# Two feature tiles to one output tile and store at the end of a decoder block, c loaded first and a shorter chain in its head

## The chip, the cores and the metric

The kernel runs on one core of one Trainium2 chip. The metric is the device time of one execution in microseconds, as the median of several runs. A core has five engines with queues of their own: PE (TensorE, matmuls), DVE (VectorE), ACT (ScalarE, activations and table lookups), POOL (GpSimd) and SP (SyncE, which in this kernel issues DMAs). Each runs its own instructions in order and waits for the others by semaphores.

## The reference

One sequence of 1024 tokens with 1024 features goes through one block in fp32. `c` is one vector of 1024 values, which conditions every norm:

```python
c_act = silu(c)
cond = c_act @ ada_w + ada_b                      # shift1, scale1, gate1, shift2, scale2, gate2
h = modulate(rmsnorm(x, norm1_g), shift1, scale1)
u, v, val, gate = split(h @ w_in + b_in)          # 512 columns each
y_a = spatial_gating_mixer(gelu(u), gelu(v), ...) # layernorm of v, 128x128 mixing in chunks
y_b = conformer_conv_mixer(val, gate, ...)        # causal depthwise conv of width 31, group norm, silu
x = x + gate1 * (concat(rmsnorm(y_a), rmsnorm(y_b)) @ w_out)
h2 = modulate(rmsnorm(x, norm2_g), shift2, scale2)
g, up = split(h2 @ w_ffn_in)
x = x + gate2 * ((silu(g) * up) @ w_ffn_out)
out = modulate(rmsnorm(x, norm_f_g), shift_f, scale_f)   # shift_f, scale_f from c_act @ ada_f_w + ada_f_b
```

## The kernel before

Features lie on the partitions and tokens along the free axis. x is held as `xs[k]`, eight feature tiles (k = 0 to 7) of 128 features by 1024 tokens, and most work goes by halves of 512 tokens (`H`). Each operand of a large matmul is split into two parts, hi and lo (`wh`, `wl`, `h[:, 0]`, `h[:, 1]`), and a product is made of three matmuls, hi by hi, lo by hi and hi by lo (`mm3`, `product`), each 128x128 by 128x512, which PE starts 0.227 us apart at full speed.

**The head.** SP loads x (first half, eight DMAs), c and the column constants (`cols`). PE broadcasts c to all partitions by two matmuls of 128x512 (line 538), ACT applies Silu (`cact`, line 539). The columns of the conditioning come from `ada_cols` (lines 549 to 559): a 512 KB tile of `ada` is loaded into a buffer (`ypad`), and DVE multiplies it by `cact` and sums each row into one column of `cond` (line 559). `rstd` (lines 631 to 661) makes 1/rms: ACT squares the tiles of x (line 641), PE sums them over features into a bank `ssq` (line 648), ACT takes the root `rt` (line 651), DVE the reciprocal (652), PE spreads it over all partitions, back into the same bank (654), and where `copy` is set ACT copies it into SBUF as `r` (660). The loop over k (line 718 on) loads the ada tiles of SCALE1 and SHIFT1 and the weights `wk[k]`, splits the weights (`wh_k` by ACT, line 586, `wl_k` by DVE, 587), finishes the two columns on ACT (722, 723) and makes h: t = x * r on DVE (725), Identity with scale and shift on ACT, in place (726), hi as a copy of t by ACT (728), lo = t - hi by DVE (729). Then 24 matmuls add this k to eight banks `p`.

**The body.** The gates, the convolution, the spatial mixer (`v`, with the scalings of `vn` in line 781; `gn`, the group norm of the convolution from `gsd`; `pm`, the mixing) and the output projection `po` follow; `ssq_b` and `rt_b` belong to the norm of the convolution's output `y_b`. After that come the FFN's two products (line 928).

**The tail.** The last norm goes by pieces: piece 0 is the first 512 tokens, pieces 1 and 2 are 256 tokens each. `square` sums squares (ACT 1204, PE 1196), `norm` makes the rstd (1225 to 1228), and `output(i)` makes each feature tile by one DVE operation (1244), one ACT operation (1246) and one store issued by SP (1247); two tiles of piece 0 go by POOL and ACT (1240 to 1242).

**What sets the order.** The program is built in the order of its text, and then `fix_order` orders the instructions of each engine anew: a planner (`Graph`, `Slots`, `Clock`, `forward`, `backward`) holds the dependences and schedules the whole by a list, with a modelled duration for each instruction (`duration`). An edge set by `issue_after` keeps an instruction behind another one. The order on each engine is fixed by what the planner's last pass gives.

Of the kernel before, what the change touches and what calls it, by code (L numbers as in the profile page):

```python
# [68 lines left out]
DMA_AHEAD = 0.5  # L69

# [54 lines left out]
def duration(s):  # L125
# [3 lines left out]
    if s.engine == "PE":  # L129
        n, m = s.writes[0].width, s.reads[1].width  # L130
        if not s.reads[0].f32:
            t = n / 512 * 0.2267
        elif n == 128:
            t = {128: 0.219, 32: 0.068}.get(m, 0.109)
        else:
            t = 0.857
        return t, t + 0.176, 0
# [34 lines left out]
class Graph:  # L172


    def __init__(self, instructions, edges, stacked, reusing):
        self.steps = []
        uses, live, tiles, order = {}, {}, {}, {}
        for ins in instructions:
# [3 lines left out]
            for operands, written in ((s.reads, False), (s.writes, True)):  # L182
                for o in operands:
# [129 lines left out]
class Clock:  # L313


    def __init__(self):
        self.free = dict.fromkeys(ENGINES, 0.0)
        self.port = self.queue = 0.0
        self.last, self.partial = None, False

    def run(self, s, t):
# [10 lines left out]
        if s.engine == "PE" and s.partial != self.partial:  # L332
            self.partial = s.partial
            t += 0.09 if s.partial else 0.12
# [20 lines left out]
def forward(g, rank):  # L355
# [7 lines left out]
    slots, clock, table = Slots(g), Clock(), None  # L363
# [17 lines left out]
    for _ in range(count):  # L381
# [21 lines left out]
        for n in s.after:  # L403
            need[n] -= 1
            same = g.steps[n].engine == e and not s.dma
            at[n] = max(at[n], (begin + s.issue if e == "PE" else end) if same else end + SIGNAL[e])
# [62 lines left out]
def block_kernel(ctx: ExitStack, tc: tile.TileContext, xT, c, ada, cols, vbias, bs, wsp,  # L469
# [161 lines left out]
    def rstd(srcs, n, name, groups, add_eng, copy=False, size=H, tmp=tmp, bank=None):  # L631
# [29 lines left out]
        return r  # L661
# [49 lines left out]
    r1a = rstd(x_half(0), D, "n1_0", (1,) * 8, None, True)  # L711
# [6 lines left out]
    for k in range(KD):  # L718
# [512 lines left out]
    def output(i, tiles=range(KD), by_pool=()):  # L1231
        bank, part = norm_banks[i], pieces[i]
        size = part.stop - part.start
        if by_pool:
            r = ev(f"r_nf{i}")[:, 0:size]
            A.activation(r, bank[:, 0:size], AF.Copy)
        for k in tiles:
            t = ev(f"of{i}_{k}")[:, 0:size]
            if k in by_pool:
                G.tensor_tensor(t, xs[k][:, part], r, op=ALU.mult)  # L1240
                A.activation(t, t, AF.Identity, bias=ccol(SHIFTF, k), scale=ccol(SCALEF, k))
                nc.sync.dma_start(out[k, :, part], t)
# [173 lines left out]
```

## Time and profile before

| | us |
|---|---|
| three runs, median | 996.74 |
| lowest, highest | 996.40, 1000.49 |
| the profiled execution, own time | 996.41 |
| its span | 994.4 |
| PE busy | 961.9 (97%) |
| DVE busy | 855.2 (86%) |
| ACT busy | 474.0 (48%) |
| POOL busy | 391.4 (39%) |

The span reaches from the first to the last recorded instruction or transfer of the profiled execution; the own time has the rest around it, 2.0 us, in it. Busy time of an engine is the sum over its instructions, registers, branches and DMA issues not counted. In the views below a line gives the start and the duration of neighbouring instructions of one kind ("x4" is four of them, and the duration is then of all four from the first start to the last end); the bracket at its end is the idle time of the engine ahead of it and what released it. "SPq" is SP issuing DMAs; 'sum' rows add the stretches.

### The profile page before, as it was taken

What the parts mean: (1) busy time and instruction counts of PE and PEld (TensorE: products, weight loads), DVE (VectorE), ACT (ScalarE), POOL (GpSimd) and SP (SyncE); (2) the same over time, 40 slices, a digit from 0 to 9 for tenths busy, and PEclk for the clock granted to TensorE, in tenths of its full rate; (3) what the DMA queues carried; (4) which work ended last, traced back from release to release, by engine and by line L of the source; (5) the groups of instructions that cost most, each with busy time, mean ns of one, the idle gap of its engine ahead of it and who ended that gap; (6) DMA issues with size and microseconds to landing.
All of it is one profiled execution on the core that took longest, in us unless ns stands there. A gap on an engine that the chain in (4) does not pass through costs nothing.

```text
span 994.4 us, 13218 instructions
## 1 busy us (share of the span) xinstructions
PE 961.9 (97%) x4645; PEld 773.6 (78%) x4645; DVE 855.2 (86%) x1197; ACT 474.0 (48%) x751; POOL 391.4 (39%) x232
## 2 busy tenths in 40 slices
PE   4999999999999999999999999999999999999994
PEld 2887777778878778888888877888887888888873
DVE  3969999999999444799999999998678989869946
ACT  6668467643484363564332332323337437236416
POOL 0037879755556111574445544445443100000121
PEclk9999999999999999999999999999999999999997
DMA  8983351524465515764677777677557838315104
GB/s 301 329 315 101 123 175 56 189 96 127 148 223 180 190 43 169 259 232 145 221 253 233 244 240 255 227 241 234 186 180 259 303 131 259 121 40 173 33 1 169
DMA packets 73667, 184.08 MB, mean 185 GB/s; under 512 B 8193, under 2 KB 10497, under 8 KB 73602
## 3 DMA queue, kind: packets, MB, share of 16 engines
q1 hardware_dynamic: 73602, 183.25, 55.6%
q8 instruction: 36, 0.59, 0.3%
q14 instruction: 29, 0.24, 0.1%
HBM read 142.06 MB, written 41.16 MB: 184 GB/s over the span
## 4 chain that ended last, share of the span: by engine, by line
PE 83%; DVE 10%; issue 2%; ACT 2%; DMA 1%; POOL 0%; SPq 0%; ACTq 0%; DVEq 0%; POOLq 0%
PE B L928 24%; PE C L928 14%; PE ah L928 11%; PE p L603 3%; PE po L603 3%; PE po L604 3%; PE po L605 3%; PE p L604 3%; PE p L605 3%; PE A L928 3%; DVE w_f L921 2%; PE v L604 2%; PE v L603 1%; PE pu L605 1%; PE v L605 1%
## 5 line engine op out<-in xcount | busy, mean ns | idle before, releaser
L928 PE MATMUL B<-h,w_f 128*128 128x512 f32 x816 | 190.8, 390 | 2.3 <-ACT x L1145 1.2
L928 PEld LDWEIGHTS B<-h,w_f 128*128 128x128 f32 x816 | 152.7, 188 | 36.4 <-DVE x L1147 3.1
L866 DVE SCALAR_TENSOR_TENSOR cv<-ypad,colt,cv 128x512 f32<-128x512 f32 x216 | 147.6, 745 | 0.5
L928 PE MATMUL B<-fa,w_d 128*128 128x512 f32 x528 | 125.5, 390 | 0.3 <-DVE x L1277 0.2
L928 PE MATMUL C<-h,w_f 128*128 128x512 f32 x528 | 123.6, 389 | 0.0
L928 PEld LDWEIGHTS B<-fa,w_d 128*128 128x128 f32 x528 | 98.8, 188 | 22.0 <-DVE x L1277 1.1
L928 PEld LDWEIGHTS C<-h,w_f 128*128 128x128 f32 x528 | 99.1, 188 | 20.6
L928 PE MATMUL ah<-h,wh_a 128*128 128x512 f32 x320 | 101.6, 395 | 0.5 <-ACT sg L673 0.5
L1209 POOL TENSOR_TENSOR sq_nf<-sq_nf,sq_nf 128x512 f32<-128x512 f32 x9 | 12.5, 1388 | 175.6 <-ACT sq_nf L1204 175.6
L920 ACT ACTIVATE w_d<-raw_d 128x512 fp32r<-128x512 f32 (+1 forms) x72 | 42.0, 593 | 83.0 <-PE B L928 34.0
L1170 POOL TENSOR_TENSOR x<-x,up 128x512 f32<-128x512 f32 x20 | 34.7, 1737 | 106.1 <-ACT x L1169 106.1
L587 POOL TENSOR_TENSOR wl_a<-raw_a,wh_a 128x1024 fp32r<-128x1024 f32 x20 | 49.2, 2461 | 67.8 <-ACT wh_a L586 57.7
L920 ACT ACTIVATE w_f<-raw_f 128x512 fp32r<-128x512 f32 x68 | 42.3, 627 | 68.4 <-PE B L928 41.6
L921 DVE TENSOR_TENSOR w_f<-raw_f,w_f 128x512 fp32r<-128x512 f32 x68 | 68.7, 1017 | 5.1 <-ACT w_f L920 5.0
L928 PEld LDWEIGHTS ah<-h,wh_a 128*128 128x128 f32 x320 | 59.9, 188 | 15.1 <-issue 1.4
L928 PE MATMUL C<-fa,w_d 128*128 128x512 f32 (+1 forms) x273 | 64.4, 384 | 0.0
L928 PE MATMUL ah<-h,wl_a 128*128 128x512 f32 x160 | 62.2, 390 | 0.0
L928 PEld LDWEIGHTS C<-fa,w_d 128*128 128x128 f32 x273 | 49.9, 188 | 11.0 <-issue 0.8
L921 DVE TENSOR_TENSOR fa<-a,fa 128x512 fp32r<-128x512 f32 x77 | 54.2, 743 | 1.7 <-ACT fa L920 1.7
L1277 DVE SCALAR_TENSOR_TENSOR x<-B,cond,x 128x512 f32<-128x512 f32 x48 | 35.6, 743 | 19.8 <-PE B L928 19.8
L920 ACT ACTIVATE fa<-a 128x512 fp32r<-128x512 f32 x77 | 46.0, 626 | 8.8 <-DMA a<-acts 5.7
L921 DVE TENSOR_TENSOR w_d<-raw_d,w_d 128x512 fp32r<-128x512 f32 (+1 forms) x72 | 47.8, 673 | 1.4 <-ACT w_d L920 1.4
(236 smaller groups left out, 2094.2 us busy)
## 6 DMA issues: line engine op xcount, KB each, us to landing
acts<-x SPq DMA_DIRECT2D x77, 256.0 KB, 3.1
a<-acts SPq DMA_DIRECT2D x77, 256.0 KB, 4.0
raw_f<-wf SPq DMA_DIRECT2D x32, 512.0 KB, 4.5
ada<-ada SPq DMA_DIRECT2D x24, 512.0 KB, 3.4
x<-ada SPq DMA_DIRECT2D x24, 512.0 KB, 3.8
raw_a<-wf SPq DMA_DIRECT2D x20, 512.0 KB, 3.8
ahead<-ahead SPq DMA_DIRECT2D x40, 256.0 KB, 3.0
ypad<-ada SPq DMA_DIRECT2D x16, 512.0 KB, 5.4
```

Of the source, the lines that this page charges most:

```text
L587: lo_eng.tensor_tensor(lo, raw, hi.bitcast(F32), op=ALU.subtract)
L603: PE.matmul(acc, shi, mhi, start=start, stop=False)
L604: PE.matmul(acc, slo, mhi, start=False, stop=False)
L605: PE.matmul(acc, shi, mlo, start=False, stop=stop)
L866: V.scalar_tensor_tensor(accs[j], src, wc, accs[j], op0=ALU.mult, op1=ALU.add)
L920: A.activation(dst[:, 0, :], src, AF.Copy)
L921: lo_eng.tensor_tensor(dst[:, 1, :], src, dst[:, 0, :].bitcast(F32), op=ALU.subtract)
L928: last_mm = PE.matmul(bank[:, cols], s, m[:, cols], start=first and p == 0 and i == 0, stop=p == n - 1 and i == 2, skip_group_check=True)
L1170: G.tensor_tensor(g0, g0, up0, op=ALU.mult)
L1209: G.tensor_tensor(sums[half], sums[half], t, op=ALU.add)
L1277: V.scalar_tensor_tensor(xs[k][:, part], bank[:, cols], ccol(GATE2, k), xs[k][:, part], op0=ALU.mult, op1=ALU.add)
```

## The change

Three things change. In `output`, two feature tiles of a piece of 256 columns share one tile of 512 columns (`row`), and one store writes both; the output in DRAM is laid out in blocks of 512 columns, (2*KD, 128, 512), and the host puts the blocks together. In the head, c is loaded first, and `issue_after(c_load)` keeps x and cols behind it on SP; `rstd` returns its bank as well as the copy, the first t reads the bank, and h's hi part is made by Identity from t directly, ahead of the Identity in place that lo needs. In the planner, the cost of a narrow fp32 matmul has another formula, PE's time is doubled where the stretch before was little active (`tensor`), PE's writes to one bank keep the order of the program, and a PE instruction's follower on PE starts from `clock.free`.

```diff
@@ duration
         if not s.reads[0].f32:
             t = n / 512 * 0.2267
-        elif n == 128:
-            t = {128: 0.219, 32: 0.068}.get(m, 0.109)
         else:
-            t = 0.857
+            k = s.reads[0].box[1] - s.reads[0].box[0]
+            t = {128: 0.219, 32: 0.068}.get(m, 0.109 if k > 64 else 0.055) * n / 128
@@ Graph
+            if s.engine == "PE":
+                if s.writes[0].name in bank:
+                    s.before.add(bank[s.writes[0].name])
+                bank[s.writes[0].name] = s.n
@@ Clock
+    def tensor(self, t, s):
+        if s.partial != self.partial:
+            self.partial = s.partial
+            t += 0.09 if s.partial else 0.12
+        w = int(t / CLOCK_WINDOW)
+        slow = 2 if self.throttled and self.active.get(w - 1, 0.0) < CLOCK_WINDOW / 2 else 1
+        end = t + slow * s.issue
...
+        self.free["PE"] = end
+        return t, t + slow * s.finish
...
-    slots, clock, table = Slots(g), Clock(), None
+    slots, clock, table = Slots(g), Clock(True), None
...
-            at[n] = max(at[n], (begin + s.issue if e == "PE" else end) if same else end + SIGNAL[e])
+            at[n] = max(at[n], (clock.free[e] if e == "PE" else end) if same else end + SIGNAL[e])
@@ block_kernel
-    nc.sync.dma_start(c_row[0:1, :], c)
+    c_load = nc.sync.dma_start(c_row[0:1, :], c).ins
     colt = const.tile([P, NCOL], F32, name="colt")
-    nc.sync.dma_start(colt, cols)
     xs = [const.tile([P, S], F32, name=f"x{k}") for k in range(KD)]
-    for k in range(KD):
-        nc.sync.dma_start(xs[k][:, hs(0)], xT[k, :, hs(0)])
+    with issue_after(c_load):
+        for k in range(KD):
+            nc.sync.dma_start(xs[k][:, hs(0)], xT[k, :, hs(0)])
+        nc.sync.dma_start(colt, cols)
@@ rstd
         A.activation(r, bank, AF.Copy)
-        return r
+        return bank[:, 0:size], r
@@ loop over k
-    r1a = rstd(x_half(0), D, "n1_0", (1,) * 8, None, True)
+    r1a_bank, r1a = rstd(x_half(0), D, "n1_0", (1,) * 8, None, True)
...
-        V.tensor_tensor(t, xs[k][:, hs(0)], r1a, op=ALU.mult)
+        V.tensor_tensor(t, xs[k][:, hs(0)], r1a_bank if k == 0 else r1a, op=ALU.mult)
+        h = h1[0][k] = act_tile(f"h1_0_{k}", 0)
+        A.activation(h[:, 0, :], t, AF.Identity, bias=ccol(SHIFT1, k), scale=ccol(SCALE1, k))
         A.activation(t, t, AF.Identity, bias=ccol(SHIFT1, k), scale=ccol(SCALE1, k))
-        h = h1[0][k] = act_tile(f"h1_0_{k}", 0)
-        A.activation(h[:, 0, :], t, AF.Copy)
         V.tensor_tensor(h[:, 1, :], t, h[:, 0, :].bitcast(F32), op=ALU.subtract)
@@ output
         size = part.stop - part.start
+        per_store = H // size
...
-            t = ev(f"of{i}_{k}")[:, 0:size]
+            if k % per_store == 0:
+                row = ev(f"of{i}_{k}")
+            t = row[:, k % per_store * size:(k % per_store + 1) * size]
...
-            A.activation(t, t, AF.Identity, bias=ccol(SHIFTF, k))
-            nc.sync.dma_start(out[k, :, part], t)
+                A.activation(t, t, AF.Identity, bias=ccol(SHIFTF, k))
+            if (k + 1) % per_store == 0:
+                nc.sync.dma_start(out[(0, KD, KD + KD // 2)[i] + k // per_store], row)
```

SP at the start of the program before: x tiles, c and cols, then the two ada tiles of k = 0 (`ypad`).

```order
L524 DMA x_76<-xT 128x512
L524 DMA x_77<-xT 128x512
L524 DMA x_78<-xT 128x512
L524 DMA x_79<-xT 128x512
L524 DMA x_80<-xT 128x512
L524 DMA x_81<-xT 128x512
L519 DMA c_row<-c 1x1024
L524 DMA x_82<-xT 128x512
L524 DMA x_83<-xT 128x512
L521 DMA colt<-cols 128x277
L554 DMA ypad_106<-ada 128x1024
L554 DMA ypad_107<-ada 128x1024
```

SP at the same place in the changed kernel.

```order
L540 DMA c_row<-c 1x1024
L576 DMA ypad_106<-ada 128x1024
L576 DMA ypad_107<-ada 128x1024
L545 DMA x_75<-xT 128x512
L545 DMA x_76<-xT 128x512
L545 DMA x_77<-xT 128x512
L545 DMA x_78<-xT 128x512
L545 DMA x_79<-xT 128x512
L545 DMA x_80<-xT 128x512
L545 DMA x_81<-xT 128x512
L545 DMA x_82<-xT 128x512
L546 DMA colt<-cols 128x277
```

c has moved from the seventh place to the first, the two ada tiles from the end to ahead of all of x, and cols to the end.

ACT in the head before, from the seventh square of x to the root: `sq_n` are the squares, `cact` the Silu of c in two halves, `rt_n` the root of the sums in the bank `ssq_n`.

```order
L641 ACTIVATE sq_n_0_6_156<-x_82 128x512
L539 ACT_TABLE_LOAD
L539 ACTIVATE cact<-c_97 128x512
L641 ACTIVATE sq_n_0_7_162<-x_83 128x512
L539 ACTIVATE cact<-c_100 128x512
L696 ACTIVATE vsel<-colt 128x1
L542 ACT_TABLE_LOAD
L542 ACTIVATE warm<-epst 128x1
L651 ACTIVATE rt_n_0_168<-ssq_n_0_119,epst 128x128
```

ACT from the start of the changed kernel to the second square.

```order
L561 ACT_TABLE_LOAD
L561 ACTIVATE cact<-c_97 128x512
L561 ACTIVATE cact<-c_100 128x512
L663 ACTIVATE sq_n_0_0_120<-x_75 128x512
L564 ACT_TABLE_LOAD
L564 ACTIVATE warm<-epst 128x1
L663 ACTIVATE sq_n_0_1_126<-x_76 128x512
```

Silu with its table has moved from between the last squares to ahead of the first, and the table for the root from behind the last square to behind the first; one of three table loads is gone. The other six squares and three small operations follow, then `rt_n`.

ACT at the first h before: `wh_k` are the hi parts of the weights, `r_n` the copy of the bank, `h_0_0` the hi part of h for k = 0.

```order
L586 ACTIVATE wh_k_193<-raw_k_191 128x1024
L660 ACTIVATE r_n_0_175<-ssq_n_0_119 128x512
L722 ACTIVATE cond<-cond,gain,colt 128x1
L726 ACTIVATE t_h_0_0_199<-t_h_0_0_199,cond 128x512
L586 ACTIVATE wh_k_235<-raw_k_233 128x1024
L728 ACTIVATE h_0_0_202<-t_h_0_0_199 128x512
```

ACT at the same place in the changed kernel, from the root on.

```order
L673 ACTIVATE rt_n_0_168<-ssq_n_0_119,epst 128x128
L608 ACTIVATE wh_k_193<-raw_k_191 128x1024
L682 ACTIVATE r_n_0_175<-ssq_n_0_119 128x512
L749 ACTIVATE h_0_0_201<-t_h_0_0_199,cond 128x512
L750 ACTIVATE t_h_0_0_199<-t_h_0_0_199,cond 128x512
```

`h_0_0` has moved ahead of the Identity in place and of the second `wh_k`, and is made from `t_h_0_0` as DVE left it.

DVE in the changed kernel from the reciprocal on, with the semaphores that each instruction waits for (`Activation` is ACT's).

```order
L674 RECIPROCAL rt_n_0_168<-rt_n_0_168 128x128 [waits Activation_49]
L609 TENSOR_TENSOR wl_k_194<-raw_k_191,wh_k_193 128x1024 [waits DMAHW4_49,Activation_49]
L747 TENSOR_TENSOR t_h_0_0_199<-x_75,ssq_n_0_119 128x512 [waits Activation_49]
L581 SCALAR_TENSOR_TENSOR ypad_108,cond<-ypad_108,cact 128x1024 [waits DMAHW5_49]
L581 SCALAR_TENSOR_TENSOR ypad_109,cond<-ypad_109,cact 128x1024 [waits DMAHW6_49]
```

The first t reads `ssq_n` where it read `r_n`; it stands ahead of an ada product (108) that stood ahead of it, and waits for ACT alone.

PE at the start of the output projection of `y_b` before, where `ssq_b` are the sums and `rt_b` the roots of its norm.

```order
L605 MATMUL po_2_3163<-y_a_2_2562,wh_o_2_3157 128x512
L648 MATMUL ssq_b_3092<-sq_b_0_3093,ones 32x128 x4
L603 MATMUL po_2_3163<-y_a_3_2567,wh_o_2_3157 128x512
L604 MATMUL po_2_3163<-y_a_3_2567,wl_o_2_3158 128x512
L605 MATMUL po_2_3163<-y_a_3_2567,wh_o_2_3157 128x512
L654 MATMUL ssq_b_3092<-rt_b_3108,colt 128x128 x4
L603 MATMUL po_0_3161<-y_b_0_3117,wh_o_0_3145 128x512
L604 MATMUL po_0_3161<-y_b_0_3117,wl_o_0_3146 128x512
```

PE at the same place in the changed kernel.

```order
L625 MATMUL po_2_3163<-y_a_2_2562,wh_o_2_3157 128x512
L626 MATMUL po_2_3163<-y_a_2_2562,wl_o_2_3158 128x512
L627 MATMUL po_2_3163<-y_a_2_2562,wh_o_2_3157 128x512
L625 MATMUL po_2_3163<-y_a_3_2567,wh_o_2_3157 128x512
L626 MATMUL po_2_3163<-y_a_3_2567,wl_o_2_3158 128x512
L676 MATMUL ssq_b_3092<-rt_b_3108,colt 128x128 x4
L627 MATMUL po_2_3163<-y_a_3_2567,wh_o_2_3157 128x512
L625 MATMUL po_0_3161<-y_b_0_3117,wh_o_0_3145 128x512
```

The sums (`ssq_b<-sq_b`) have moved ahead: they stand 14 rows before the spread of `rt_b` now, with 13 po between, where 3 stood, and one po has moved behind the spread.

In the rest of PE's order, the first `gn<-gsd` stands at row 529 (before 550) and the first `pm<-wt,vn` at 548 (before 554); PE changes between narrow fp32 matmuls and full ones 68 times (before 72). SP's last stores are eight of 128x512 for pieces 1 and 2 (before sixteen of 128x256).

## Rows read from the trace of the kernel before

**Rows 1.** Stretches: length, each engine's busy time, PEclk, DMA share, GB/s.

```profile
0.00:24.20 24.20, 10.94 (x76) 4.58 (x76) 8.89 (x16) 15.32 (x25) 0.49 (x8) 1.00 0.86 302
...
31.20:200.00 168.80, 168.80 (x942) 132.62 (x940) 158.36 (x234) 111.47 (x168) 113.66 (x62) 1.00 0.53 181
...
978.00:994.40 16.40, 2.31 (x18) 1.32 (x16) 10.22 (x21) 10.63 (x24) 2.50 (x2) 0.67 0.63 217
sum 994.40, PE 961.86 PEld 773.65 DVE 855.25 ACT 473.96 POOL 391.40; mean PE 96.19 PEld 77.36 DVE 85.52 ACT 47.40 POOL 39.14
```

**Rows 2.** Timeline of ACT, 0 to 25 us, and 85.4 to 88.4.

```profile
7.89 2.71 ACT L641 ACTIVATE sq_n<-x 128x512 f32<-128x512 f32 x4 [1.61 <-DMA x<-xT]
10.61 1.28 ACT L539 ACT_TABLE_LOAD   x1
...
16.61 0.35 ACT L651 ACTIVATE rt_n<-ssq_n,epst 128x128 f32<-128x128 f32 x1
...
20.54 0.60 ACT L660 ACTIVATE r_n<-ssq_n 128x512 f32<-128x512 f32 x1 [1.76 <-PE ssq_n L654]
...
21.89 0.81 ACT L726 ACTIVATE t_h<-t_h,cond 128x512 f32<-128x512 f32 x1 [0.29 <-DVE t_h L725]
...
85.52 1.66 ACT L641 ACTIVATE sq_n<-x 128x512 f32<-128x512 f32 x3
```

**Rows 3.** Timeline of DVE, 14 to 27 us.

```profile
17.43 0.95 DVE L652 RECIPROCAL rt_n<-rt_n 128x128 f32<-128x128 f32 x1
18.81 1.23 DVE L587 TENSOR_TENSOR wl_k<-raw_k,wh_k 128x1024 fp32r<-128x1024 f32 x1 [0.44 <-ACT wh_k L586]
...
21.16 0.69 DVE L725 TENSOR_TENSOR t_h<-x,r_n 128x512 f32<-128x512 f32 x1
```

**Rows 4.** Timeline of PE, 8 to 28 us.

```profile
11.80 0.66 PE L648 MATMUL ssq_n<-sq_n,ones 128*32 128x128 f32 x8
...
18.43 2.08 PE L654 MATMUL ssq_n<-rt_n,colt 128*128 128x128 f32 x8 [2.95 <-DVE rt_n L652]
24.22 0.80 PE L603 MATMUL p<-h,wh_k 128*128 128x512 f32 x1 [3.72 <-ACT h L728]
```

**Rows 5.** Timeline of PE, 361.7 to 367 us.

```profile
363.98 1.16 PE L654 MATMUL ssq_b<-rt_b,colt 128*128 128x128 f32 x8 [0.58 <-DVE rt_b L652]
366.64 0.50 PE L603 MATMUL po<-y_b,wh_o 128*128 128x512 f32 x1 [1.50 <-ACT y_b L824]
```

**Rows 6.** Timeline of ACT, 974 to 995 us.

```profile
983.70 6.47 ACT L1246 ACTIVATE of<-of,cond 128x256 f32<-128x256 f32 x16
```

**Rows 7.** Timeline of SP, 974 to 995 us.

```profile
984.24 7.81 SPq L1247 DMA_DIRECT2D out<-of  x16
```

**Rows 8.** DMA issues, 972 to 995 us: KB each, median us to landing.

```profile
out<-of SPq DMA_DIRECT2D x8, 256.0 KB, 2.1
out<-of SPq DMA_DIRECT2D x16, 128.0 KB, 1.9
```

**Rows 9.** The chain that ended last, 940 to 994.4 us, in order of time.

```profile
959.55 2.04 PE B L928 x9
...
961.94 2.27 PE C L928 x9
```

**Rows 10.** Timeline of DVE and PE, 145 to 158 us; line L781's durations (min/median/max ns).

```profile
147.01 0.92 DVE L897 RECIPROCAL gsd<-gsd 128x128 f32<-128x128 f32 x1
147.85 5.63 DVE L781 TENSOR_SCALAR vn<-vn,mv,sd 128x512 f32<-128x512 f32 x4
...
153.38 1.97 PE L901 MATMUL gn<-gsd,colt 128*64 128x128 f32 x32
...
155.94 1.97 PE L807 MATMUL pm<-wt,vn 128*64 128x128 f32 x32
...
L781 DVE TENSOR_SCALAR vn<-vn,mv,sd x8: 448/1412/2464, 147.8 to 186.7; 128x512 f32<-128x512 f32 x8
```

**Rows 11.** Timeline of PE, 972 to 975 us.

```profile
972.80 1.05 PE L1228 MATMUL ssq_nf<-rt_nf,colt 128*128 128x128 f32 x8
```

More of the change, by code (lines that the diff above doesn't have):

```diff
@@ L69 @@
 DMA_AHEAD = 0.5
+CLOCK_WINDOW = 3.4133
 class Step:
@@ L176, in __init__ @@
         self.steps = []
-        uses, live, tiles, order = {}, {}, {}, {}
+        uses, live, tiles, order, bank = {}, {}, {}, {}, {}
         for ins in instructions:
@@ L313, with __init__ @@
 class Clock:
-    def __init__(self):
+    def __init__(self, throttled=False):
         self.free = dict.fromkeys(ENGINES, 0.0)
@@ L319, in __init__ @@
         self.last, self.partial = None, False
+        self.throttled, self.active = throttled, {}
+    def tensor(self, t, s):
[5 more added lines that the diff above has]
+        end = t + slow * s.issue
+        a = t
+        while a < end:
+            w = int(a / CLOCK_WINDOW + 1e-9)
+            b = min(end, (w + 1) * CLOCK_WINDOW)
+            self.active[w] = self.active.get(w, 0.0) + b - a
+            a = b
+        self.free["PE"] = end
+        return t, t + slow * s.finish
     def run(self, s, t):
@@ L331, in run @@
             self.port = t + s.port
-        if s.engine == "PE" and s.partial != self.partial:
-            self.partial = s.partial
-            t += 0.09 if s.partial else 0.12
+        if s.engine == "PE":
+            return self.tensor(t, s)
         self.free[s.engine] = t + s.issue
@@ L1241, in output @@
                 A.activation(t, t, AF.Identity, bias=ccol(SHIFTF, k), scale=ccol(SCALEF, k))
-                nc.sync.dma_start(out[k, :, part], t)
-                continue
-            V.scalar_tensor_tensor(t, xs[k][:, part], ccol(SCALEF, k), bank[:, 0:size],
-                                   op0=ALU.mult, op1=ALU.mult)
-            A.activation(t, t, AF.Identity, bias=ccol(SHIFTF, k))
-            nc.sync.dma_start(out[k, :, part], t)
+            else:
+                V.scalar_tensor_tensor(t, xs[k][:, part], ccol(SCALEF, k), bank[:, 0:size],
+                                       op0=ALU.mult, op1=ALU.mult)
+                A.activation(t, t, AF.Identity, bias=ccol(SHIFTF, k))
+            if (k + 1) % per_store == 0:
+                nc.sync.dma_start(out[(0, KD, KD + KD // 2)[i] + k // per_store], row)
     DESTS = {1: (0, 0), 2: (0, 0), 5: (4, 1), 7: (4, 1), 6: (0, 1), 3: (0, 1), 4: (4, 0)}
@@ L1409 @@
             for k, v in arrays.items()]
-    args.append(nc.dram_tensor("out", (KD, P, S), F32, kind="ExternalOutput").ap())
+    args.append(nc.dram_tensor("out", (2 * KD, P, H), F32, kind="ExternalOutput").ap())
     with tile.TileContext(nc, schedule_with_timeline_sim=True) as tc:
@@ L1414 @@
     o = r.results[0]["out"]
+    o = np.concatenate([o[:KD], o[KD:].reshape(2, KD // 2, P, 2, H // 2).transpose(1, 3, 2, 0, 4).reshape(KD, P, H)],
+                       axis=2)
     return np.ascontiguousarray(o.reshape(D, S).T).reshape(1, S, D)
```

## The prediction

> **What bounds the kernel now.** I read the stretches first [rows 1]. TensorE (PE) is busy 961.86 of 994.40 us. Before 24.20 us it is busy for 10.94, after 978.00 for 2.31, so of the 953.80 us between it works 961.86 − 10.94 − 2.31 = 948.61: 5.2 us of idle time in the whole body. Time can come from three places: the head (24.2 us until the stream of full matmuls starts), those 5.2 us, and the end after PE (16.4 us). VectorE (DVE) is next: 158.36 of 168.80 us in the stretch from 31.2 to 200.
>
> Then the head, engine by engine. Four squares starting at 7.89, after a wait of 1.61 for x, come (2.71 − 0.63)/3 = 0.69 us apart; squares whose data are there come (1.66 − 0.63)/2 = 0.52 apart. At 10.61 a table load for Silu, 1.28 us, stands between the squares, and the order shows a second one, for Sqrt, behind the last [rows 2]. From there it is one chain over three engines: rt at 16.61, reciprocal 17.43 for 0.95, PE's spread 18.43 for 2.08, copy of r 20.54 for 0.60, t 21.16 for 0.69, Identity 21.89 for 0.81, a weight copy and the hi copy, and PE starts the first p at 24.22, after 3.72 us of waiting for that copy [rows 2 to 4].
>
> In the body, one wait lies where the order changes visibly, at b_out(1): rt_b's spread waits 0.58 us for the reciprocal, and the next po 1.50 for y_b [rows 5].
>
> Last the end: 16 half-width ACT operations from 983.70 for 6.47 us, to 990.17, 0.40 apart, and 16 stores issued by SP from 984.24 for 7.81, to 992.05, 0.49 apart [rows 6, 7]. Issuing is slower than what feeds it and ends last. A store of 128 KB lands about 1.9 us after its issue [rows 8], and that ends the span.
>
> **The change part by part.** The sum is made against the profiled execution's 996.41 us, which is 2.0 over its span and 0.3 below the median of 996.74.
>
> *Head.* c goes first on SP, and the new order puts two 512 KB ada loads ahead of x, so 1 MB lands before x0. In the trace 1 MB, four tiles of 256 KB, was there at 7.89; one tile more is 0.69, and c's issue ahead of all about 0.3 (SP's issues are 0.49 apart at the end): x0 at 8.9. Both broadcasts of c and both Silu need only c and are over by then: off the path, at nothing; if c came as late as x0, they would put two broadcasts ahead of the first square. Then one square (0.63): 9.5; the Sqrt table (1.28): 10.8; the warm-up, about 0.1; seven squares 0.52 apart, the last 0.63 long: 14.7. At 0.69 apart x7 lands at 8.9 + 4.8 = 13.7 and is squared by 14.4, so ACT sets the pace. PE's last sums, 0.66 as at 11.80: 15.4. rt and its handover 0.4: 15.8. Reciprocal 0.95: 16.8. Spread 2.08: 18.9. Copy 0.60: 19.5. t 0.69: 20.3. Identity straight into hi, 0.81: 21.15. Against 24.22 that is **−3.1 us**. Some 1.5 of it is the stretch from 21.89 to 24.22 (Identity, weight copy, hi copy), which becomes one Identity; the rest is the earlier rt, 15.4 for 16.61. Bounds: −2.0 if x0 lands 1.1 later (the 1.61 of waiting before 7.89 shows gaps of that size), −4.6 if x0 is there 1.5 earlier, at 7.4, and the rest of x keeps up.
>
> *The bank read.* The first t reads r from the bank instead of ACT's copy. That saves nothing: in the new order it waits for ACT alone, so it stands behind the 0.60 us copy of the same bank. I count 0; if it ran beside the copy, 0.6 more, which the bound of −4.6 takes in. The Trainium skill, "PSUM — Partial Sum Buffer", section "PSUM bank collisions raise a hardware error", says that two engines may not access the same bank and partitions at once, two readers included; by it the copy and t must follow each other and the head gives 3.1, where the edit as written would give 3.7. No row of before has two such readers.
>
> *Hidden.* The second Identity (t for the lo part) and DVE's lo are first needed by the matmuls with h's lo half, several full matmuls into the first k. In the steady state DVE needs two ada products and wl, 1.23 each, and t and lo, 0.69 each, 5.07 us for a k, less than PE's 24 × 0.227 = 5.45. If that cover is gone the gain of the head comes back as waits for h (third rival).
>
> *b_out(1).* Where 3 po stood between ssq_b and rt_b's spread there are 13 now, then one po, then y_b's. The 0.58 is filled, and one po of 0.227 stands in the 1.50: **−0.8**. Bounds 0 (if ssq_b's squares are late as well) and −2.1 (both waits).
>
> *Switches between narrow and full matmuls.* Nine full ones behind narrow ones take 2.27 us instead of 2.04 [rows 9]: 0.23 a return. The new order has 68 changes of kind for 72, two returns less: **−0.45**, bounds 0 and −0.5.
>
> *Tail.* 16 stores become 8 of 256 KB. SP then issues one for every two ACT operations, 0.80 apart, more than its 0.49, so the last issue begins 0.1 after ACT's end at 990.17 and not at 992.05 − 0.40 = 991.65: −1.4. The larger store lands 2.1 us after its issue, not 1.9 [rows 8]: +0.25 with its longer tail. **−1.15**, bounds −0.9 and −1.5.
>
> *The rest of the order* moves with the planner's costs. At the spatial mixer gn stands 21 rows earlier on PE, 21 × 0.227 = 4.8 us; its input was ready at 147.93 and it ran at 153.38, so 0.6 of slack remains. pm stands 6 rows earlier, 1.4 us; its last input was ready at 153.48 and it ran at 155.94, so 1.1 remains [rows 10]. Cost 0, under a thin cover.
>
> Sum: −3.1 − 0.8 − 0.45 − 1.15 = −5.5, span 988.9, time **990.9 us**.
>
> **The rivals.**
> 1. *PE runs at its full clock in the head already.* The head's spread took 2.08 us; the tail's, of the same form and count, 1.05 [rows 4, 11]: by their durations the levels of 1.2 and 2.4 GHz, though the column of the granted clock says 1.00 for the head and 0.67 for the end [rows 1]; I go by the durations. The new head's sums come closer together; were the rate full by then, the spread would save 1.0, and the first 8 full matmuls, at half rate now, 8 × 0.2 = 1.6: 988.3. Against it: the sums and broadcasts ahead of 18.43, eight of them from 11.80, left that spread at the lower level, and the new order still leaves PE idle around it. Chance 0.10. The Trainium skill, "TensorE: Matmul & The Clock Gate", says that sustained activity releases the lower rate; by that alone it would come out at 988.3, and the trace shows the spread at the lower level with sums right ahead of it.
> 2. *The loads take back half of the head.* x comes after 1 MB and shares the way with cols and weights. If x0 lands 1.5 later than reckoned, the head gives 1.6: 992.4. For it: loads at the start come with gaps (1.61 before the square at 7.89). Against: no byte is added ahead of the last x but 1 MB of ada, and ACT has 0.3 to spare. Chance 0.20.
> 3. *DVE keeps its old times.* It is 94% busy from 31.2 to 200; if its work there does not start earlier with PE, the head's 3.1 returns as waits of PE in that stretch, and 0.8 + 0.45 + 1.15 = 2.4 remain: 994.0. Against: PE waited for nothing there, and DVE has 10 us to spare. Chance 0.12.
> 4. *Slower: pm, moved up, waits for the scalings.* The four scalings of vn took 5.63 us where one takes from 0.45 to 2.46 [rows 10]. At 2.46 each they end 4.2 later; less the 1.1 of slack PE stands 3.1 us, in both halves 6.2, more than the 5.5 gained: 997.1. It decides from 2.75 us a half. Chance 0.06.
>
> That the shared store does nothing (another engine ends last) is 1.15 less gain, 992.1, within the forecast's own range.
>
> **How the numbers follow.** Forecast 0.52, rivals 0.10, 0.20, 0.12, 0.06. The likeliest is 990.9, by the bounds 989.2 to 992.8. To hold 8 in 10 the range takes in rivals 1 to 3: 988.0 to 995.0, and leaves out rival 4 and the ends. A measurement of this kernel tells some 0.5%, 5.0 us, from no change, so "faster" begins at 991.76. Seven in ten of the forecast lie under that, all of rival 1, a quarter of rival 2, little of rival 3: 0.52. Slower by 5 us has only rival 4 with something on top: 0.04. The same: 0.44.
>
> **What would show it.** In the new profile: the first p near 21.2 us, and t behind the copy of r; the sums of PE all after 9 us and the c broadcasts before; no wait of rt_b's spread, and 1.2 to 1.3 us for y_b; 0.5 us less of full matmuls behind narrow ones; SP's last store right behind ACT's last operation, and 3 us between its begin and the span's end. The prediction is wrong if x0 lands after 10.4, if PE shows new waits for gn, pm or h behind the first k, or if ACT's half-width operations come further apart than 0.40.

## The result, and the profile after

The changed kernel takes 989.65 us in the median (988.89 to 991.20, four runs); beside it, with its new runs, the kernel before takes 998.62 (996.40 to 1000.78, four runs). The ratio is 0.9922, with a 95% interval from 0.9902 to 0.9941: faster by 0.8%. One of six later executions of the changed kernel took 2489.77 us and is left out of every comparison here. Of the two profiled executions the one before took 996.41 and the one after 990.04, with spans of 994.4 and 988.3. Forecast were 990.9 and a span of 988.9, reckoned from the profiled 996.41 less 5.5; the profiled executions differ by 6.4, the medians by 9.0.

The stretches of the changed kernel, as in [rows 1] (length, each engine's busy time, granted clock, DMA share, GB/s):

```profile
0.00:21.20 21.20, 12.16 (x80) 6.00 (x81) 8.13 (x15) 13.41 (x23) 0.49 (x8) 1.00 0.90 333
...
974.00:988.30 14.30, 1.83 (x12) 1.18 (x12) 9.38 (x20) 10.28 (x24) 2.50 (x2) 0.60 0.63 231
sum 988.30, PE 960.96 PEld 774.25 DVE 862.28 ACT 474.23 POOL 399.54; mean PE 106.77 PEld 86.03 DVE 95.81 ACT 52.69 POOL 44.39
```

PE is busy 960.96 us, about as long as before (961.86), so 5.2 of the 6.1 us of span came out of idle time, and that at the ends: head and end hold 21.5 us of it (27.4 before), the body between them 5.8 (5.2 before). ACT in the head after:

```profile
6.18 0.60 ACT L561 ACTIVATE cact<-c 128x512 f32<-128x512 f32 x1 [1.11 <-PE c L560]
6.98 0.63 ACT L663 ACTIVATE sq_n<-x 128x512 f32<-128x512 f32 x1 [0.20 <-DMA x<-xT]
7.63 1.28 ACT L564 ACT_TABLE_LOAD   x1
...
9.03 3.92 ACT L663 ACTIVATE sq_n<-x 128x512 f32<-128x512 f32 x7
...
13.72 0.37 ACT L673 ACTIVATE rt_n<-ssq_n,epst 128x128 f32<-128x128 f32 x1 [0.22 <-PE ssq_n L670]
...
17.25 0.60 ACT L682 ACTIVATE r_n<-ssq_n 128x512 f32<-128x512 f32 x1 [2.21 <-PE ssq_n L676]
18.60 0.81 ACT L749 ACTIVATE h<-t_h,cond 128x512 fp32r<-128x512 f32 x1 [0.76 <-DVE t_h L747]
```

DVE:

```profile
14.12 0.95 DVE L674 RECIPROCAL rt_n<-rt_n 128x128 f32<-128x128 f32 x1 [1.36 <-ACT rt_n L673]
...
17.88 0.69 DVE L747 TENSOR_TENSOR t_h<-x,ssq_n 128x512 f32<-128x512 f32 x1 [1.58 <-ACT r_n L682]
```

and PE:

```profile
15.13 2.08 PE L676 MATMUL ssq_n<-rt_n,colt 128*128 128x128 f32 x8 [1.48 <-DVE rt_n L674]
19.47 0.80 PE L625 MATMUL p<-h,wh_k 128*128 128x512 f32 x1 [2.26 <-ACT h L749]
...
24.67 0.40 PE L625 MATMUL p<-h,wh_k 128*128 128x512 f32 x1
```

These answer to [rows 2 to 4]. One table load stands inside the chain (7.63), the seven squares from 9.03 come 0.55 apart without a wait, and the steps behind them take what the forecast gave them: the reciprocal starts 0.40 after rt, the spread takes 2.08, t starts 0.63 after the copy, and p starts 0.87 after h does. The first p starts at 19.47, where 21.15 was forecast and 24.22 was measured before. But 11 p and not 8 are 0.43 apart; from 24.67 on they are 0.23 apart.

The waits of PE in the body (sum in us, times, longest):

```profile
PE po L625 <- ACT y_b L846: 1.3, 1, 1.3
PE ssq_b L670 <- POOL sq_b L667: 1.1, 2, 0.7
```

The 0.58 us of rt_b's spread at b_out(1) [rows 5] is gone, and 1.3 us for y_b remains. The wait for POOL at `ssq_b` is new.

The end, ACT's half-width operations:

```profile
978.83 6.47 ACT L1270 ACTIVATE of<-of,cond 128x256 f32<-128x256 f32 x16
```

the last piece of the chain that ended last:

```profile
984.50 0.80 ACT of L1270 x2
```

and the stores of the tail (KB each, median us to landing):

```profile
out<-of SPq DMA_DIRECT2D x16, 256.0 KB, 2.1
```

ACT's sixteen operations take the same 6.47 us as in [rows 6] and end at 985.30, and the chain ends in them: SP's last store follows ACT and lands 2.1 us later. From the first of them to the end of the span it is 988.3 − 978.83 = 9.47 us; before it was 994.4 − 983.70 = 10.70.

Both programs hold 3,933 full matmuls, and the n-th of one does the same job as the n-th of the other but for small moves. Its start in each trace less its start in the trace of before shows where time comes and goes. The table is worked out from the traces; the last two lines are from the timeline of ACT and the span, and the columns other than the second are experiments, told below (the last is head and tail with five fillers, its first run).

| matmul, its start before | after | tail only | head only | planner only | head and tail | the same, filled |
|---|---|---|---|---|---|---|
| 1st, first p, 24.22 | −4.75 | −0.34 | −4.60 | +2.11 | −4.23 | −5.60 |
| 13th, 28.74 | −4.06 | +0.14 | −3.83 | +2.86 | −4.07 | −7.26 |
| 241st, 80.42 | −4.05 | +0.17 | −3.55 | +7.14 | −4.06 | −7.26 |
| 401st, 122.79 | −3.13 | +0.01 | −4.15 | +7.05 | −4.68 | −7.87 |
| 541st, 164.89 | −2.96 | +0.01 | −4.14 | +7.05 | −4.67 | −7.86 |
| 761st, 229.58 | −1.92 | +0.01 | −5.21 | +7.38 | −5.77 | −8.95 |
| 1181st, 331.15 | −1.93 | −0.02 | −5.22 | +7.38 | −5.81 | −8.99 |
| 1301st, 370.43 | −2.62 | +1.47 | −5.18 | +6.74 | −5.78 | −7.35 |
| 3701st, 922.30 | −4.94 | +0.17 | −4.63 | +5.81 | −6.42 | −6.90 |
| half-width ACT, 983.70 | −4.87 | +0.47 | −4.63 | +5.81 | −6.13 | −6.61 |
| end of the span, 994.4 | −6.1 | −0.8 | −4.6 | +5.9 | −7.4 | −7.8 |

### The profile page after: what moved, and what is told of

It reads as the page before. It is cut to its first block, busy times and chain, and to the rows that moved or that the text cites. A ratio compares the mean times of both kernels' runs of the same rounds, so it can differ in the third digit from the quotient of the medians.

```text
span 988.3 us, 13193 instructions
## 1 busy us (share of the span) xinstructions
PE 961.0 (97%) x4645; PEld 774.3 (78%) x4645; DVE 862.3 (87%) x1197; ACT 474.2 (48%) x750; POOL 399.5 (40%) x232
## 4 chain that ended last, share of the span: by engine, by line
PE 81%; DVE 10%; ACT 4%; issue 2%; DMA 1%; POOL 1%; SPq 0%; ACTq 0%; DVEq 0%; POOLq 0%
PE B L950 28%; PE C L950 16%; PE ah L950 11%; DVE cv L888 4%; PE A L950 3%; PE po L625 3%; PE po L626 3%; PE po L627 3%; PE p L627 3%; PE p L625 3%; PE p L626 3%; PE pm L829 1%; PE gn L923 1%; DVE w_f L943 1%; DVE x L581 1%
## 5 line engine op out<-in xcount | busy, mean ns | idle before, releaser
L943 DVE TENSOR_TENSOR w_f<-raw_f,w_f 128x512 fp32r<-128x512 f32 x68 | 65.6, 970 | 3.5 <-ACT w_f L942 3.4
```

The source lines that it names most:

```text
L943: lo_eng.tensor_tensor(dst[:, 1, :], src, dst[:, 0, :].bitcast(F32), op=ALU.subtract)
```

## The experiments

Theory: the gain is the head's and the tail's, by the mechanisms of the forecast; the body carries the head's gain to the end. Rivals: the planner's new costs made it; or the gain depends on how the first loads land. Ten kernels in twelve runs tell these apart. Each edit is planned anew, so it also moves the order on the engines elsewhere. Ratios are to runs of the kernel before on the same chip.

**The tail alone.** The kernel before with the hunk of `output` and the host's layout.

```diff
+            t = row[:, k % per_store * size:(k % per_store + 1) * size]
...
+            if (k + 1) % per_store == 0:
+                nc.sync.dma_start(out[(0, KD, KD + KD // 2)[i] + k // per_store], row)
```

> The kernel before with only the shared output tile and store. Theory (SP's issuing ends last): from the first half-width ACT operation to the end of the span 9.5 us instead of 10.7, the first full matmul of p still near 24.2 us, and 1.2 us less in all, some 995.2 for a profiled 996.4. Rival (landing or ACT ends the span, and the shorter end of the changed kernel came from the planner's order): 10.5 us or more from that ACT operation to the end, and no gain.

996.60 us against 998.52, ratio 0.9976 (0.9961 to 0.9990). ACT at the end, of a span of 993.6:

```profile
984.17 6.47 ACT L1248 ACTIVATE of<-of,cond 128x256 f32<-128x256 f32 x16
```

From 984.17 to 993.6 it is 9.43 us, where the kernel before takes 10.70: the shared stores give 1.27, as the theory said. The profiled total fell by 0.8 only, since the body came 0.47 later to that point: behind the waits at b_out(1), which are those of before, the first seven po are 0.43 apart (granted clock 0.58 from 366.5 to 370.5 us), and between the 1181st and the 1301st matmul 1.49 us is lost that the kernel before did not lose. That is this execution's clock and not the edit.

**The head alone.** The kernel before with the hunks of the head, planned by the old costs.

```diff
+    with issue_after(c_load):
...
+        V.tensor_tensor(t, xs[k][:, hs(0)], r1a_bank if k == 0 else r1a, op=ALU.mult)
+        h = h1[0][k] = act_tile(f"h1_0_{k}", 0)
+        A.activation(h[:, 0, :], t, AF.Identity, bias=ccol(SHIFT1, k), scale=ccol(SCALE1, k))
```

> The kernel before with only the changes of the head (c first, hi from t, first t from the bank), planned by the old costs. Theory (the head's gain is the changes of the text, and PE carries most of it to the end): first p at 19.3 to 19.8 us, and some 4 us less in all, 992.4. Rival (it needs the new planner, or the body takes it back): first p above 21, or a gain under 2 us.

991.54 us, ratio 0.9923 (0.9904 to 0.9942), the ratio of the whole change. First p at 24.22 − 4.60 = 19.62, and 4.63 of that is still there at the first half-width ACT operation. The head needs no new planner.

**The planner alone.** The kernel before with the hunks ahead of `block_kernel`.

```diff
-    slots, clock, table = Slots(g), Clock(), None
+    slots, clock, table = Slots(g), Clock(True), None
```

> The kernel before with only the planner's new costs. Theory (the planner's part is small): first p between 24.0 and 24.6 us, the place of b_out(1) 0.7 us shorter, the waits of the first norm of y_b some 1 us longer, in all within 1.2 us of before, 995.2 to 997.6. Rival (the planner made a third or more of the gain): 994.0 or less.

1002.05 us, ratio 1.0043 (1.0027 to 1.0060): slower. Neither side was right. Its two large waits of PE before 200 us:

```profile
PE p L624 <- ACT h L749: 5.1, 1, 5.1
...
PE pu L624 <- ACT sg L694: 2.4, 1, 2.4
```

The first was 3.7 in [rows 4], the second did not exist. With the old head, the new costs put two ada products of DVE ahead of the first t (the order has one there before), so p starts 2.11 later, 0.7 of it with rt, at 17.35 for 16.61, since the loads came later; by the 241st matmul another 4.3 is lost from the 13th on, 2.4 of it in the wait of `pu` for the gate and some 1.6 behind it, where eight pu are 0.43 apart (granted clock 0.52 from 76 to 79.5 us). So part of the loss of this execution is the clock, not the order.

**No bank read.** The changed kernel, t reading ACT's copy.

```diff
-        V.tensor_tensor(t, xs[k][:, hs(0)], r1a_bank if k == 0 else r1a, op=ALU.mult)
+        V.tensor_tensor(t, xs[k][:, hs(0)], r1a, op=ALU.mult)
```

> The changed kernel, but the first t reads ACT's copy of r and not the bank. Theory (t stands behind the copy either way): t starts within 0.15 us of the copy's end as in the changed kernel, first p at 19.3 to 19.7, time within 0.7 us of the changed kernel, 989.3 to 990.7. Rival (reading the bank saves the copy's 0.6 us): first p at 20.0 or later.

989.08 us, ratio 0.9899 (0.9880 to 0.9919), no worse than with the read. ACT:

```profile
9.74 4.79 ACT L663 ACTIVATE sq_n<-x 128x512 f32<-128x512 f32 x7 [0.51 <-DMA x<-xT]
...
18.83 0.60 ACT L682 ACTIVATE r_n<-ssq_n 128x512 f32<-128x512 f32 x1 [2.21 <-PE ssq_n L676]
...
20.18 0.81 ACT L749 ACTIVATE h<-t_h,cond 128x512 fp32r<-128x512 f32 x1 [0.49 <-DVE t_h L747]
```

From the copy's start to h it is 20.18 − 18.83 = 1.35 us; with the bank read it is 18.60 − 17.25 = 1.35. The read is worth nothing, as forecast. The expected 19.3 to 19.7 for the first p failed for another reason. The tiles behind the first came later: the squares from 9.74 waited for data and took 4.79 us where the changed kernel's took 3.92, so all behind them is 1.6 later, p at 21.05. The kernel is as fast all the same: its body gained 2.1 us between the first p and the 3,701st matmul, where the changed kernel's gained 0.2.

**Head and tail under the old planner.** Both sets of hunks above, none of the planner's.

> The changed kernel with the old planner, that is the head and the shared stores alone. Theory (head and tail add up, and the planner's part is near nothing beside the new head): first p at 19.4 to 19.9 us, the end 9.5 us behind the first half-width ACT operation, 991.54 less 1.25 is 990.3, within 1 us of the changed kernel. Rival (the new planner is needed with the new head): 991.5 or more.

989.17 us, ratio 0.9916 (0.9899 to 0.9933): as fast as the whole change, and the profiled span (987.0) is shorter. Head and tail are the change; its new planner adds nothing that shows here.

**x ahead of every ada tile.** The changed kernel with all later DMAs of SP behind x.

```diff
+            x_last = nc.sync.dma_start(xs[k][:, hs(0)], xT[k, :, hs(0)]).ins
...
+    edges.extend((i.name, x_last.name) for i in nc.cur_bb.bb.instructions[n_loads:]
+                 if i.engine == x_last.engine and type(i) is type(x_last))
```

> The changed kernel, with every other load of SP behind the last load of x, so that no ada tile lands ahead of x. Theory (the head is set by when x lands, then by ACT's pace of squares): squares run between and right behind the two Silu, the last ends near 11 instead of 12.95, first p at 17.0 to 18.0 us, and 1.5 to 2 us less in all, 988. Rival (ACT's chain behind c is the limit, or ada now lands too late): first p at 19 or later and no gain.

994.00 us, ratio 0.9960 (0.9945 to 0.9975), 4 us slower than the changed kernel; the theory fell. ACT in its head:

```profile
9.47 0.63 ACT L664 ACTIVATE sq_n<-x 128x512 f32<-128x512 f32 x1 [1.71 <-DMA x<-xT]
10.12 1.28 ACT L565 ACT_TABLE_LOAD   x1
...
11.53 2.17 ACT L664 ACTIVATE sq_n<-x 128x512 f32<-128x512 f32 x4
```

The fourth square waits until 9.47 though no ada tile is ahead of it, the table load stands behind it, the last square ends at 13.70 (12.95 in the changed kernel), and p starts at 20.22, 0.75 later. What came in from 3 to 7 us in this kernel (GB/s in the last column):

```profile
3.00:5.00 2.00, 2.00 (x3) 0.66 (x2) 0.00 (x0) 0.57 (x2) 0.00 (x0) 1.00 0.84 288
5.00:7.00 2.00, 2.00 (x18) 0.59 (x16) 0.00 (x0) 1.47 (x4) 0.00 (x0) 1.00 0.89 234
```

and in the changed kernel, where ada tiles come first:

```profile
3.00:5.00 2.00, 2.00 (x3) 0.66 (x2) 0.00 (x0) 0.53 (x1) 0.00 (x0) 1.00 1.01 371
5.00:7.00 2.00, 1.15 (x2) 0.00 (x0) 0.19 (x1) 0.69 (x3) 0.00 (x0) 1.00 1.00 328
```

x goes in tiles of 256 KB with 2 KB a row, ada in tiles of 512 KB with 4 KB a row. With x first 288 and 234 GB/s come in, with ada first 371 and 328, so more bytes are there by 7 us. Size of tile, length of row and order of the loads change together here; which of them does it isn't shown.

Most of the 4 us is lost elsewhere. PE's sums for the second half of x waited 2.3 us for ACT's squares in this order, behind that wait six pu were 0.43 apart (granted clock 0.54 from 86 to 89 us), and between the 241st and the 281st matmul (−3.93 to +0.26) all of the head's gain was gone.

**t ahead of the copy.** The changed kernel, the copy of r issued behind the first t.

```diff
+        if k == 0:
+            A.activation(r1a, r1a_bank, AF.Copy)
```

> The changed kernel with ACT's copy of r placed behind the first t, so that t reads the bank alone and first. Theory (the copy's 0.60 us is what t stood behind): t starts right behind PE's spread, first p 0.5 to 0.7 us earlier against the spread's end than in the changed kernel (2.27 us from the spread's end to p there), and 0.5 less in all. Rival (the copy then stands ahead of h on ACT and holds it): the same 2.27 us or more.

990.68 us, ratio 0.9926 (0.9910 to 0.9943). ACT:

```profile
18.85 0.60 ACT L748 ACTIVATE r_n<-ssq_n 128x512 f32<-128x512 f32 x1 [2.93 <-DVE t_h L746]
19.35 0.80 ACT L750 ACTIVATE h<-t_h,cond 128x512 fp32r<-128x512 f32 x1
```

Now the copy waits for t (2.93 us idle, put down to DVE) and stands ahead of h: the two readers still go one after the other. From the spread's end (18.10) to p it is 2.11 us, not 2.26: 0.15 of the 0.60. The theory (0.5 to 0.7) fell, the rival was right in the main. In all nothing is gained; in this execution x came later than in the changed kernel's (first square at 7.54), and p began at 20.20.

**PE filled ahead of p.** The changed kernel with eight matmuls whose result p overwrites.

```diff
+    with issue_after(last["rstd"]):
+        for _ in range(8):
+            PE.matmul(acc[(3, 1)][:, 0:P], ones.broadcast_to([P, P]), xs[7][:, 0:P], start=True, stop=True)
```

> The changed kernel with eight idle narrow matmuls (128x128, into a bank that p overwrites) on PE between the spread of r and the first p, where PE waits 2.3 us. Theory (PE's clock stays at its lower level in the first p because PE sat idle before them; it cost 11 matmuls at 0.43 instead of 0.227): the first p start at the same time or up to 0.2 later, fewer than 7 of them are 0.43 apart, and 0.8 to 2 us less by the twelfth. Rival (work ahead of p does not raise the clock): 10 or more at 0.43, and no gain.

993.74 us, ratio 0.9961 (0.9946 to 0.9977). PE:

```profile
19.74 3.48 PE L739 MATMUL p<-x,ones 128*128 128x128 f32 x16 [1.41 <-DVE t_h L750]
22.97 0.47 PE L625 MATMUL p<-h,wh_k 128*128 128x512 f32 x1
```

The place was badly chosen: this bank is the one that holds r, so the fillers waited for t and ran when p was due. But behind them every p but the first is 0.23 apart: PE's clock was up. So of the 3.5 us that p starts later than in the changed kernel 1.1 is left at the 13th matmul (−2.92 for −4.06). The kernel is 4 us slower in the medians and 2.3 in the profiled spans (990.6 for 988.3); `gn` has a new wait of 2.4.

**Filled early.** Five fillers into a free bank.

```diff
+        for _ in range(5):
+            PE.matmul(acc[(2, 0)][:, 0:P], ones.broadcast_to([P, P]), xs[7][:, 0:P], start=True, stop=True)
```

> The changed kernel with five idle narrow matmuls (128x128) between the spread of r and the first p, into a bank that is free by then, so that they run while PE waits and not after. Theory (the level of PE's clock in the first p follows from what PE did before them; in the run with eight fillers every p but the first was 0.23 apart): fillers run at once behind the spread, 0.43 each, 2.2 us; first p 2.2 to 2.5 us behind the spread's end as without them; the thirteenth p 5.2 to 6.5 us behind the spread's end and not 7.47; 1 to 2 us less by there. Rival (the fillers only take the time that they save): 7.2 us or more.

989.61 us, ratio 0.9912 (0.9886 to 0.9938). PE:

```profile
15.64 2.07 PE L676 MATMUL ssq_n<-rt_n,colt 128*128 128x128 f32 x8 [1.47 <-DVE rt_n L674]
17.51 2.34 PE L739 MATMUL p<-x,ones 128*128 128x128 f32 x10
19.97 0.80 PE L625 MATMUL p<-h,wh_k 128*128 128x512 f32 x1
20.57 0.48 PE L626 MATMUL p<-h,wl_k 128*128 128x512 f32 x1
20.89 0.40 PE L625 MATMUL p<-h,wh_k 128*128 128x512 f32 x1
```

The fillers run right behind the spread, p starts 2.26 us behind its end as without them, and two matmuls are slow, not 11. The thirteenth starts 5.5 us behind the spread's end (it was 7.47), so 2 us are saved there. This order has a new wait of 1.5 us of p for the gate. The profiled span is 986.6, 1.7 less than the changed kernel's, but the runs (988.41 to 991.50) do not tell the two apart.

**Head, tail and the five fillers, old planner**, twice; the second time beside the changed kernel on one chip.

The edit is the hunks of head and tail with the five fillers of the last diff. For the first time it was expected:

> Head and shared stores under the old planner, with the same five fillers. Theory (nothing in the body waits on the fillers, and PE carries the gain to the end): 1 to 2 us less than the 989.17 of head and stores without them, 987.2 to 988.2. Rival (the body takes it back, or its order moves): 989 or more.

For the changed kernel, with no edit, beside the second:

> The changed kernel once more, unchanged, beside the next one. Theory (the head's gain hangs on when x0 lands, which varies by some tenths from run to run; the rest of the order is fixed): first square of x between 6.8 and 7.6 us, first p 12.5 us behind it (as 6.98 and 19.47), place of the first y_b norm 1.1 us of waits for POOL again, time 989.0 to 990.5. Rival (those waits and the 11 slow p were accidents of one execution): no wait there, or fewer than 9 slow p.

And for the second:

> Head and shared stores under the old planner with five fillers once more, on the same chip as the changed kernel. Theory (denser work of PE in the head is what raised its clock): the spread of r takes 1.2 us again where its sums come within 4.8 us, at most two slow p, and 1.0 to 1.8 us less than the changed kernel beside it. Rival (the full clock at the spread was an accident, the fillers give little): spread 2.1 us, and less than 0.8 us between the two.

988.22 us at first, ratio 0.9898 (0.9875 to 0.9922). PE in that execution:

```profile
9.03 4.69 PE L649 MATMUL ssq_n<-sq_n,ones 128*32 128x128 f32 x64 [2.72 <-ACT sq_n L642]
15.21 1.16 PE L655 MATMUL ssq_n<-rt_n,colt 128*128 128x128 f32 x8 [1.49 <-DVE rt_n L653]
...
18.62 0.50 PE L604 MATMUL p<-h,wh_k 128*128 128x512 f32 x1 [1.14 <-ACT h L731]
```

The spread took 1.16 us, not 2.08: the clock was up before it and before the fillers, and all p ran at full speed. At the second time the changed kernel took 990.35 (ratio 0.9925, 0.9905 to 0.9944) and this one 989.44 (0.9920, 0.9899 to 0.9941). PE again:

```profile
16.21 2.07 PE L655 MATMUL ssq_n<-rt_n,colt 128*128 128x128 f32 x8 [1.47 <-DVE rt_n L653]
...
20.54 0.80 PE L604 MATMUL p<-h,wh_k 128*128 128x512 f32 x1
...
21.56 0.43 PE L604 MATMUL p<-h,wh_k 128*128 128x512 f32 x1
```

Here the spread is at the lower level again and two p are slow. So the fillers take away the slow p, and the fast spread came in one of fourteen profiles; what it hangs on isn't settled. 0.9 us in one pair of medians is not a sure gain where the intervals overlap.

The two executions of this one program differ at b_out(1) too. Both wait 0.58 us for rt_b and 1.57 for y_b there. Behind the waits po ran on at 0.23 apart in the second, but in the first execution seven po were 0.43 apart, with the clock that this row shows (0.55, third number from the end):

```profile
358.20:362.00 3.80, 3.80 (x12) 2.94 (x11) 3.10 (x6) 1.38 (x3) 0.00 (x0) 0.55 0.00 0
```

From the 1181st to the 1301st matmul the first lost 1.6 us by it (−8.99 to −7.35 in the table), the second nothing.

Of the changed kernel's second profile, ACT:

```profile
6.97 0.63 ACT L663 ACTIVATE sq_n<-x 128x512 f32<-128x512 f32 x1
...
9.03 4.45 ACT L663 ACTIVATE sq_n<-x 128x512 f32<-128x512 f32 x7
```

The first square is at 6.97 as before, but the seven behind it took 4.45 us for 3.92, waiting for x; p began at 19.98, 13.0 behind the first square and not 12.5, 12 p were slow, and POOL's 1.1 us was there again. The wait for POOL belongs to the order; the load's half microsecond belongs to the run.

## Why the prediction was right, and which terms were mis-sized

The mechanisms held and the time lay 1.3 us below the forecast, with errors of both signs. That it came so near has luck in it. The forecast took 5.5 us from 996.41, one of the fastest executions of the kernel before; the medians beside each other differ by 9.0 us, and by 7.6 in the later pair (997.94 and 990.35). No trace of a slower execution of before was taken, so what it loses there stays open. Nor do the bounds of the terms give the range of 989.2 to 992.8: added up they give 987.7 to 993.5.

*The head*, forecast −3.1, measured −4.75 (from −3.17 to −4.75 over the kernels with this order of loads and without fillers; the bound was −4.6). From the root to the first p it takes 5.75 us, as forecast (7.61 before), and every step behind the first square was sized to within 0.2 us. The step that failed is "In the trace 1 MB … was there at 7.89; one tile more is 0.69 … x0 at 8.9": it took the landing of the fourth tile for the time that 1 MB needs. x0 was squared at 6.98. What came in before (GB/s in the last column), and the square of the third tile, right behind its landing:

```profile
3.00:5.00 2.00, 0.62 (x8) 0.20 (x8) 0.00 (x0) 0.84 (x2) 0.00 (x0) 1.00 0.86 293
5.00:7.00 2.00, 1.35 (x20) 0.40 (x16) 0.00 (x0) 1.05 (x2) 0.00 (x0) 1.00 0.91 274
...
5.64 0.63 ACT L641 ACTIVATE sq_n<-x 128x512 f32<-128x512 f32 x1 [0.23 <-DMA x<-xT]
```

With 98 GB/s up to 3 us, 1.43 MB had come by 7 us, but only three tiles, 0.79 MB, had landed. In the changed kernel 1.56 MB had come by then (55 GB/s up to 3 us, then 371 and 328), and 1.31 MB had landed: two tiles of ada and x0. So the kernel before had bytes of the later tiles under way when the fourth landed, and that gap is most of the error; the higher rate is the smaller part. In the traces ada's tiles land at 4.98 and 6.28 and x0 0.68 behind, the forecast's own price of one tile. Once four tiles of x are there, the next land 0.65 to 0.68 us apart before, and two tiles of ada 1.28: by their sizes an estimate of 390 and 410 GB/s. The Trainium skill, "DMA: Bandwidth & Descriptors", section "Bandwidth", says that larger transfers come nearer to the peak. The rows up to 7 us agree in direction, the later landings show little of it.

The second rival wanted x0 later than 8.9; it landed between 6.95 and 7.52 in all kernels with these loads. Without the bank read the tiles behind it came late and took 1.6 us. With the early x0 one sign of the forecast fell too: PE's sums began at 7.67 and not after 9. The third rival's waits for h behind the first k did not come.

*The bank read*, forecast 0, measured 0 (1.35 us from the copy to h with it and without). The order of t and copy is a queue, not a saving: turned round, it gives 0.15.

*The first p*, forecast to stay at 8 slow matmuls, measured 11: 0.70 of the head's gain was given back by the 13th matmul. It was not in the sum. How much of it belongs to the new head isn't shown: the count is 8 before, 10 with the same head and only the tail changed, 11 and 12 in two executions of the changed kernel, and 8 to 13 over the ten profiles without fillers. In the four profiles with fillers it is 0 to 2, so work of PE ahead of p takes the slow matmuls away. The Trainium skill, "TensorE: Matmul & The Clock Gate", Part 1, says that activity releases the lower rate and that the number of matmuls at that rate at a start varies from run to run; the traces agree, with 11 and 12 in two executions of one program, 0 and 2 in two of another, and there a spread of 1.16 and of 2.07. Rival 1's condition, the full clock at the spread, came in one of the fourteen profiles.

*b_out(1)*, forecast −0.8, measured −0.69 from the 1181st to the 1301st matmul (−1.93 to −2.62). The step was right: all eight profiles with the new planner gain 0.64 to 0.69 there. With the old one it is 0.03 of loss, or 1.5 and 1.6 where the clock fell.

*The rest of the order*, forecast −0.45 for the switches and 0 for the other moves; measured from the first p to the first half-width ACT operation −0.12 in all. Between lie +0.70 (clock), +0.92 near 90 us, +0.17 at the mixer, +1.04 near 210 us, −0.69 (b_out), and −2.32 in the rest, the FFN nearly all. Of the largest loss the waits tell the cause: PE's first sums for `ssq_b` stand 24 matmuls earlier in its order, ahead of what POOL delivers. POOL before:

```profile
202.21 2.41 POOL L587 TENSOR_TENSOR wl_o<-raw_o,wh_o 128x1024 fp32r<-128x1024 f32 x1 [2.57 <-ACT wh_o L586]
204.58 2.98 POOL L645 TENSOR_TENSOR sq_b<-sq_b,sq_b 128x512 f32<-128x512 f32 x2
```

and after:

```profile
199.82 2.82 POOL L609 TENSOR_TENSOR wl_o<-raw_o,wh_o 128x1024 fp32r<-128x1024 f32 x1 [1.24 <-DVE ypad L697]
202.61 4.48 POOL L667 TENSOR_TENSOR sq_b<-sq_b,sq_b 128x512 f32<-128x512 f32 x2
```

Before, POOL was done with both squares at 207.56, and PE came to its first sums at 213.06. After, POOL is done at 207.09, but PE is there from 204.26 on and waits 0.66 and 0.44. The order of PE is the larger part; besides, the split ahead takes 2.82 us and not 2.41 and each square 2.24 and not 1.49, and why POOL is slower there isn't shown. "Cost 0, under a thin cover" was thus wrong in place: the cover that tore was neither gn's nor pm's. Under the old planner, head and tail lose nothing there (−4.67 to −5.77): by the 761st matmul they are 3.85 us ahead of the changed kernel, by the 3,701st 1.48, since b_out and the FFN gain 3.0 in the changed order and 0.65 in the other. What gave 2.3 us in the FFN, in this order and in that without the bank read, isn't settled: its waits stand at other matmuls in each kernel, and the forecast's 0.45 can't be told apart in them.

*The tail*, forecast −1.15, measured −1.23, and −1.27 alone. Right, by the mechanism: SP's issue no longer ends last, ACT does.

*The slower rival* (pm and gn) did not come; the waits of `gn` and `pm` after are under 0.2. That gn's cover is thin shows in the kernel with eight fillers, where `gn` waits 2.4. Where the head was old, the planner's new costs did bring a loss: 3.5 us in the medians, 5.9 in the profiled spans.

## What to carry to other kernels

The landing of the n-th of several loads is not the time that its bytes need, since loads behind it are under way beside it: count the bytes that had come by then. Reckon a gain from the median and not from the one profiled execution, which may be a fast one. When a scheduler's costs change along with the code, time the code under the old costs too: here all of the gain was the code's, and the new costs alone made the old code slower. A wait of PE can cost more than its length, since in some executions the clock falls behind it. A gain at the head arrives at the end only through every in-order queue behind it, so follow the difference matmul by matmul and not by the sum of waits.

## What had not been expected of the hardware

The same program ran the eight matmuls of the spread in 1.16 us in one execution and in 2.07 in another, with 64 sums ahead of it over 4.69 us in the first and over 5.9 in the second; with the head alone they came over 4.96 and the spread took 2.08. In the head the column of the granted clock stood at 1.00 while matmuls were 0.43 apart [rows 1, 4], so there only durations tell the level. In the body the column does tell it: in four of the fourteen profiles it fell to 0.52 to 0.58 behind waits of 1.5 to 2.4 us, at b_out(1) twice, where other executions with the same waits kept 1.00. Runs of one kernel spread by 2 to 3 us (988.7 to 991.2 for the changed one), and two profiled executions of it differ by 0.9 in the span, 0.5 of it from when the seven tiles of x behind the first landed.
